# Moving the stationary operands of a float32r matmul stream by multiples of 32 bytes

## The chip, the cores and the metric

The kernel runs on one core of a Trainium2 chip. The metric is device time in microseconds (us) for one execution of the whole program, from the host's launch to its end. The profile has a span of its own, from the first to the last instruction on the core.

## What is computed

Two layers of a streaming encoder on 256 tokens of width 2048, in float32. Each layer has one wide projection, three groups of attention-like heads on parts of it, an output projection, two layer norms and a SwiGLU feed-forward part.

```python
for li in range(DEPTH):                                   # DEPTH = 2, x: (1, 256, 2048)
    proj = x @ w_in[li]                                   # 2048 -> 6920 columns
    ...                                                   # split into the three groups
    ya = diff_attention(qa, ka, va, lam[li], subln_a[li], li)
    yb = chunk_band_attention(qb, kb, vb, rel_bias[li])
    yc = mlstm(qc, kc, vc, oc, ic, fc, conv_w[li], norm_c[li])
    mix = jnp.concatenate([ya, yb, yc], axis=-1) @ w_out[li]
    x = layer_norm(DEEPNORM_ALPHA * x + mix, ln1_g[li], ln1_b[li])
    ffn = (jax.nn.silu(x @ w_gate[li]) * (x @ w_up[li])) @ w_down[li]   # D_FF = 5632
    x = layer_norm(DEEPNORM_ALPHA * x + ffn, ln2_g[li], ln2_b[li])
```

## The kernel before, in words

The four large products (w_in, w_out, w_gate with w_up, w_down) are one long stream of matmuls. `run_groups` cuts it into groups of up to 1024 output columns and each group into steps `k` of 128 rows of the weights. float32 accuracy is kept by splitting each operand in two float32r parts, high and low, and adding three products: high times high, high times low and low times high.

- **Weights (moving operand).** `load_pair` brings two steps at a time from memory into a `raw` tile; `convert` makes the high part `whi` on ScalarE (line 225) and the low part `wlo` on VectorE (line 226). Each has six buffers of 128 partitions x 4096 bytes.
- **Input (stationary operand).** The 256 rows of x, or of the mixed heads, are transposed on TensorE (line 296, `tr_block`) and split by `split` (lines 286 and 287) into `xth` and `xtl`. One pair of tiles holds four steps of 128 rows; `new_xt` (line 290) hands out four slots for each of the two, in turn. So a group of 16 steps uses each slot for four steps in a row.
- **SwiGLU product (stationary operand of w_down).** It lies in `gth` and `gtl`, 24576 bytes per partition each (line 1029), with a tile `gpad` of `G_PAD` float32 ahead of them (line 1028).

Line 273 is the matmul of the stream. A step has, for each of two token halves `t`, three products times two column blocks of 512 (in one group of each layer 512 and 264): twelve matmuls, each with its own weight load of 128 columns. In the rows, `mm<-whi,xth` names first the moving and then the stationary operand. The small matmuls and transposes of attention (`aux` tiles) stand in the same TensorE queue between two steps.

Where tiles lie. Each pool takes a stretch of every partition's bytes, in the order in which the pools are opened: constants, x, the slots of `xth` and `xtl`, then `raw`, `whi`, `wlo`, then small tiles, then the pools of a layer's attention or feed-forward part. Before the change every slot of `xth` and `xtl`, every buffer of `whi` and `wlo`, and `gth` and `gtl` start at 32 modulo 256 bytes. Inside a tile the operands start at multiples of 512 bytes. What is called distance below is the address of the stationary operand less that of the moving operand beside whose matmul it is loaded, modulo 256: in the stream of before it is 0 throughout. The operands of attention lie elsewhere. With `whi` as the matmul's moving operand the distance of the load behind it is 192 for `eT` (line 750), `work` (line 742) and `g_a` (line 493, four columns), 96 for the triangle of ones (line 484), 0 for `x` (line 296), 128 for `mixc` in the first layer and 160 in the second (line 296), and 4 for the `qk` tile that line 626 loads at 352.50 us.

Work that runs beside the stream (evacuations, layer norms, attention's steps) is put between steps by `Tasks`, by fixed costs in the code.

Of the kernel before, what the change touches and what calls it, by code (L numbers as in the profile page):

```python
# [10 lines left out]
F32 = mybir.dt.float32  # L11
F32R = mybir.dt.float32r
# [5 lines left out]
P = 128  # L18
SEQ = 256
# [26 lines left out]
FAR_AHEAD = 4  # L46
EVAC_ACT = (0, 1)
LAST_SKEW = 6
G_PAD = 32
WARM = 9  # L50
MM_BUFS = 5
AUX_BUFS = 3
# [23 lines left out]
class Tasks:  # L76
# [4 lines left out]
    def __init__(self):  # L81
        self.q = []
        self.credit = 0.0
# [52 lines left out]
class Trunk:  # L136
    def __init__(self, tc, ctx, x, w_in, gate_bias, conv_w, lam, subln_a, norm_c, rel_bias, w_out,
                 ln1_g, ln1_b, w_gate, w_up, w_down, ln2_g, ln2_b, cst, out):
        self.tc, self.nc, self.ctx = tc, tc.nc, ctx
        self.__dict__.update(x=x, w_in=w_in, gate_bias=gate_bias, conv_w=conv_w, lam=lam, subln_a=subln_a,  # L140
                             norm_c=norm_c, rel_bias=rel_bias, w_out=w_out, ln1_g=ln1_g, ln1_b=ln1_b,
                             w_gate=w_gate, w_up=w_up, w_down=w_down, ln2_g=ln2_g, ln2_b=ln2_b, cst=cst, out=out)
        self.tasks = Tasks()
        pool = lambda name, bufs=1, **kw: ctx.enter_context(tc.tile_pool(name=name, bufs=bufs, **kw))
        self.const = pool("const")
        self.res = pool("res")
        self.xtp = pool("xtp")
        self.wp = pool("wp")
        self.small = pool("small", bufs=4)
        self.psum = pool("psum", space=bass.MemoryType.PSUM)  # L150
        self.flags = set()
        self.cms = {}


# [132 lines left out]
        self.nc.vector.tensor_tensor(out=lo, in0=ps, in1=hi.bitcast(F32), op=ALU.subtract)  # L287

    def new_xt(self):
        return [self.xtp.tile([P, 4, SEQ], F32R, name=n, tag=n, bufs=4) for n in ("xth", "xtl")]  # L290

    def tr_block(self, srcs, dst, slot0, t):

# [722 lines left out]
    def ffn_groups(self, l):  # L1016
        groups = []
        box = {}
        for hf in range(2):
            blk0 = sum(FF_SPLIT[:hf])  # L1020
            for bi in range(FF_SPLIT[hf]):
# [4 lines left out]
                def start(hf=hf, bi=bi):  # L1026
                    if bi == 0:
                        self.gpool.tile([P, G_PAD], F32, name="gpad")
                        self.gt = [self.gpool.tile([P, KH, SEQ], F32R, name=n, tag=n) for n in ("gth", "gtl")]
# [96 lines left out]
```

## Time and profile before

| | |
|---|---|
| device time, median of 2 runs | 2342.24 us (2341.36 to 2343.12) |
| the profiled execution's own time | 2341.18 us |
| its span | 2339.4 us |
| mean granted TensorE clock | 0.998 |
| matmuls on TensorE, busy | 2318.4 us, 10538 instructions |
| weight loads, busy (they overlap matmuls) | 1905.5 us |
| VectorE, ScalarE, GpSimd busy | 1498.3, 1034.5, 55.1 us |
| DMA | 441.15 MB, mean 189 GB/s |

The busy time of an engine is the union of its instructions' times. Matmuls are pipelined: one starts before the one ahead of it has ended, and the ends are modelled, so the pace is read from starts, and the duration of one matmul moves with the distance from its start to the next. "x2" in a timeline row is two instructions merged. In the groups, "mean ns of one" is the mean duration, then comes the idle time of the engine ahead of them.

### The profile page before, as it was taken

To read this page: it belongs to the slowest core of one execution; us is meant where nothing else is said; L and a number is where in the kernel's file an instruction comes from. 1 tells how busy PE (TensorE), PEld (TensorE's weight loads), DVE (VectorE), ACT (ScalarE), POOL (GpSimd) and SP (SyncE) were. 2 spreads that over 40 slices of the span, in tenths; PEclk is the share of its full clock that TensorE was granted. 3 is DMA by queue.
4 is the path that set the end of the run, shared out by engine and by line. 5 is a ranking of instruction groups with operands and counts; after the bars stand their busy time and mean duration, and the time that the engine had idled before them with its cause. 6 is when DMAs were issued, how large, how long until landed. Compare 5 with 4: busy or idle time off the path is not lost.

```text
span 2339.4 us, 27628 instructions
## 1 busy us (share of the span) xinstructions
PE 2318.4 (99%) x10538; PEld 1905.5 (81%) x10538; DVE 1498.3 (64%) x2360; ACT 1034.5 (44%) x1303; POOL 55.1 (2%) x120
## 2 busy tenths in 40 slices
PE   9999999999999999999999999999999999999997
PEld 7887788888888888888888877888888888888886
DVE  5755455777766447766577454557677664577765
ACT  5645554444444334444345454544444433444432
POOL 0001200000000000000000021000000000000000
PEclk9999999999999999999999999999999999999999
DMA  8654345565555555555556544555655555556553
GB/s 280 202 187 168 133 164 201 185 224 181 194 201 197 196 188 192 186 207 189 177 182 212 182 144 152 172 198 200 209 185 198 198 192 190 193 180 212 184 196 109
DMA packets 178933, 441.15 MB, mean 189 GB/s; under 512 B 15120, under 2 KB 22256, under 8 KB 177776
## 3 DMA queue, kind: packets, MB, share of 16 engines
q1 hardware_dynamic: 178656, 439.32, 55.5%
q8 instruction: 82, 1.34, 0.2%
q14 instruction: 51, 0.42, 0.1%
q10 hardware_dynamic: 144, 0.07, 0.0%
HBM read 437.25 MB, written 2.10 MB: 188 GB/s over the span
## 4 chain that ended last, share of the span: by engine, by line
PE 96%; DVE 2%; POOL 1%; ACT 1%; DMA 0%; issue 0%; SPq 0%; POOLq 0%
PE mm L273 92%; PE aux L296 1%; PE aux L543 1%; PE aux L415 1%; POOL mixc L610 1%; DVE x L341 0%; PE aux L716 0%; PE aux L626 0%; DVE bst L320 0%; DMA raw<-w_in 0%; ACT whi L225 0%; POOL rs L332 0%; POOL ve L330 0%; DVE wlo L226 0%; PE aux L750 0%
## 5 line engine op out<-in xcount | busy, mean ns | idle before, releaser
L226 DVE TENSOR_TENSOR wlo<-raw,whi 128x1024 fp32r<-128x1024 f32 (+2 forms) x817 | 985.8, 1212 | 705.0 <-ACT whi L225 700.9
L225 ACT CAST whi<-raw 128x1024 fp32r<-128x1024 f32 (+2 forms) x817 | 852.6, 1045 | 1172.5 <-PE mm L273 1142.9
L273 PE MATMUL mm<-whi,xth 128*128 128x512 f32 (+1 forms) x2560 | 812.6, 392 | 0.5 <-ACT whi L225 0.3
L273 PE MATMUL mm<-wlo,xth 128*128 128x512 f32 (+1 forms) x2560 | 799.1, 387 | 0.0
L273 PE MATMUL mm<-whi,xtl 128*128 128x512 f32 (+1 forms) x2560 | 798.2, 387 | 0.0
L273 PEld LDWEIGHTS mm<-whi,xtl 128*128 128x128 f32 x2560 | 476.2, 188 | 100.0 <-DVE xtl L287 0.6
L273 PEld LDWEIGHTS mm<-wlo,xth 128*128 128x128 f32 x2560 | 476.5, 188 | 98.8
L273 PEld LDWEIGHTS mm<-whi,xth 128*128 128x128 f32 x2560 | 467.0, 188 | 96.3 <-issue 4.0
L273 PE MATMUL mm<-whi,gtl 128*128 128x512 f32 x704 | 222.0, 389 | 0.0
L273 PE MATMUL mm<-whi,gth 128*128 128x512 f32 x704 | 222.0, 389 | 0.0
L273 PE MATMUL mm<-wlo,gth 128*128 128x512 f32 x704 | 221.9, 389 | 0.0
L407 DVE STREAM_TRANSPOSE gtr<-sil 32x128 f32<-32x128 f32 x704 | 213.0, 303 | 11.2
L273 PEld LDWEIGHTS mm<-whi,gth 128*128 128x128 f32 x704 | 132.1, 188 | 27.7
L273 PEld LDWEIGHTS mm<-whi,gtl 128*128 128x128 f32 x704 | 132.1, 188 | 27.5
L273 PEld LDWEIGHTS mm<-wlo,gth 128*128 128x128 f32 x704 | 132.1, 188 | 27.3
L330 POOL TENSOR_SCALAR ve<-mv 128x1 f32<-128x1 f32 x8 | 4.7, 590 | 1756.6 <-DVE mv L328 1756.5
L286 ACT CAST xth<-aux 128x512 fp32r<-128x512 f32 (+1 forms) x58 | 28.8, 511 | 29.0 <-PE aux L296 25.6
L287 DVE TENSOR_TENSOR xtl<-aux,xth 128x512 fp32r<-128x512 f32 (+1 forms) x58 | 33.5, 592 | 4.3 <-ACT xth L286 4.0
L1088 DVE TENSOR_TENSOR gtl<-gtr,gth 128x512 fp32r<-128x512 f32 x44 | 29.9, 681 | 0.7
L1035 ACT ACTIVATE sil<-mm 128x512 f32<-128x512 f32 x44 | 25.9, 594 | 9.9 <-PE mm L273 9.9
L1038 DVE TENSOR_TENSOR sil<-mm,sil 128x512 f32<-128x512 f32 x44 | 28.2, 682 | 1.4 <-ACT sil L1035 1.4
L341 DVE SCALAR_TENSOR_TENSOR x<-x,rs,lnb 128x512 f32<-128x512 f32 (+1 forms) x40 | 24.7, 639 | 2.8 <-POOL rs L332 2.7
(154 smaller groups left out, 677.1 us busy)
## 6 DMA issues: line engine op xcount, KB each, us to landing
raw<-w_gate SPq DMA_DIRECT2D x176, 512.0 KB, 3.7
raw<-w_up SPq DMA_DIRECT2D x176, 512.0 KB, 4.6
raw<-w_down SPq DMA_DIRECT2D x88, 1024.0 KB, 5.1
raw<-w_in SPq DMA_DIRECT2D x78, 1024.0 KB, 4.9
raw<-w_out SPq DMA_DIRECT2D x32, 1024.0 KB, 5.2
raw<-w_in SPq DMA_DIRECT2D x52, 512.0 KB, 4.1
raw<-w_in SPq DMA_DIRECT2D x16, 256.0 KB, 3.9
lng<-ln_g SPq DMA_DIRECT2D x4, 1024.0 KB, 7.8
```

Source lines behind the costliest of these rows:

```text
L225: nc.scalar.copy(out=hi[:, s], in_=src[:, s])
L226: nc.vector.tensor_tensor(out=lo[:, s], in0=src[:, s], in1=hi[:, s].bitcast(F32), op=ALU.subtract)
L273: nc.tensor.matmul(banks[t, b][:, 0:w], lt, wt[:, o:o + w], start=(k == 0 and i == 0), stop=(k == nk - 1 and i == 2))
L286: self.nc.scalar.copy(out=hi, in_=ps)
L287: self.nc.vector.tensor_tensor(out=lo, in0=ps, in1=hi.bitcast(F32), op=ALU.subtract)
L296: self.nc.tensor.transpose(out=ps[:, i * P:(i + 1) * P], in_=s, identity=self.ident)
L341: nc.vector.scalar_tensor_tensor(out=z, in0=z, scalar=rs, in1=lb[:, s], op0=ALU.mult, op1=ALU.add)
L407: self.nc.vector.transpose(out=out[32 * j:32 * j + 32, 0:n, 32 * i:32 * i + 32], in_=in_[32 * i:32 * i + 32, 0:n, 32 * j:32 * j + 32])
L415: self.nc.tensor.transpose(out=ps[:, i * P:(i + 1) * P], in_=stg[:, i * P:(i + 1) * P], identity=self.ident)
L1035: nc.scalar.activation(out=box["s", t], in_=bank, func=AF.Silu)
L1038: nc.vector.tensor_tensor(out=g, in0=bank, in1=g, op=ALU.mult)
L1088: nc.vector.tensor_tensor(out=lo, in0=gt, in1=hi.bitcast(F32), op=ALU.subtract)
```

## The change

The slots of `xth` and `xtl` become 32 bytes longer each (`XT_PAD` of 8 float32), so that the four slots start 32 bytes apart modulo 256. A tile of 128 bytes that nothing uses is put between the last slot of `xth` and the first of `xtl`. `G_PAD` falls from 32 to 16 float32.

Worked out from the pools' sizes, the slots of `xth`, and those of `xtl`, then start at 32, 64, 96 and 128 modulo 256, `raw`, `whi` and `wlo` at 160, and `gth` and `gtl` at 96. The distances are 128, 160, 192 and 224 for the four slots and 192 for the two parts of the product. In a group the steps 0 to 3, 4 to 7, 8 to 11 and 12 to 15 meet distances 128, 224, 192 and 160. The order of the instructions on every engine, their shapes and what they wait for are the same as before.

```diff
-G_PAD = 32
+G_PAD = 16
+XT_PAD = 8
...
+        self.padded = False
...
     def new_xt(self):
-        return [self.xtp.tile([P, 4, SEQ], F32R, name=n, tag=n, bufs=4) for n in ("xth", "xtl")]
+        out = []
+        for n in ("xth", "xtl"):
+            x = self.xtp.tile([P, 4 * SEQ + XT_PAD], F32R, name=n, tag=n, bufs=4)
+            out.append(x[:, 0:4 * SEQ].rearrange("p (k q) -> p k q", q=SEQ))
+            if n == "xth" and not self.padded:
+                self.padded = True
+                self.xtp.tile([P, 32], F32, name="xpad")
+        return out
```

## Rows read from the trace of the kernel before

**Rows 1.** The page, engines' busy time, and TensorE's granted clock in 40 slices.

```profile
PE 2318.4 (99%) x10538; PEld 1905.5 (81%) x10538; DVE 1498.3 (64%) x2360; ACT 1034.5 (44%) x1303; POOL 55.1 (2%) x120
...
PEclk9999999999999999999999999999999999999999
```

**Rows 2.** Chain of work that ended last, in time: start us, us, what.

```profile
479.13 683.00 PE mm L273 x3012
```

**Rows 3.** Groups by line and shape, whole run: count | busy us, mean ns.

```profile
L273 PE MATMUL mm<-wlo,xth 128*128 128x512 f32 x2496 | 790.7, 390 | 0.0
...
L273 PE MATMUL mm<-whi,gth 128*128 128x512 f32 x704 | 222.0, 389 | 0.0
...
L273 PE MATMUL mm<-wlo,xth 128*128 128x264 f32 x64 | 18.1, 282 | 0.0
```

**Rows 4.** Timeline of TensorE, settled stretch: start us, us, what; first and last.

```profile
1000.07 0.62 PE L273 MATMUL mm<-whi,xth 128*128 128x512 f32 x2
...
1005.51 0.62 PE L273 MATMUL mm<-whi,xth 128*128 128x512 f32 x2
```

**Rows 5.** Groups by line and shape, 500 to 1150 us.

```profile
L273 PE MATMUL mm<-whi,xtl 128*128 128x512 f32 x628 | 196.5, 389 | 0.0
...
L273 PE MATMUL mm<-whi,gth 128*128 128x512 f32 x330 | 102.7, 389 | 0.0
```

**Rows 6.** Timeline of TensorE in the group with 264 columns, first and last.

```profile
65.71 0.51 PE L273 MATMUL mm<-whi,xtl 128*128 128x512 f32 x2
...
67.81 0.39 PE L273 MATMUL mm<-whi,xtl 128*128 128x512 f32 x1
```

**Rows 7.** Timeline of TensorE around one transpose of x.

```profile
29.74 0.62 PE L273 MATMUL mm<-whi,xtl 128*128 128x512 f32 x2
30.20 0.60 PE L296 MATMUL aux<-cst_sb,x 128*128 128x128 f32 x4
30.55 0.71 PE L273 MATMUL mm<-whi,xth 128*128 128x512 f32 x2
31.09 0.62 PE L273 MATMUL mm<-wlo,xth 128*128 128x512 f32 x2
31.56 0.62 PE L273 MATMUL mm<-whi,xtl 128*128 128x512 f32 x2
32.02 0.62 PE L273 MATMUL mm<-whi,xth 128*128 128x512 f32 x2
```

**Rows 8.** Timeline of TensorE, small matmuls that follow a main one.

```profile
119.75 0.28 PE L484 MATMUL aux<-g_lf,cst_sb 128*128 128x4 f32 x2
...
122.71 0.61 PE L273 MATMUL mm<-whi,xtl 128*128 128x512 f32 x2
123.16 0.38 PE L493 MATMUL aux<-cst_sb,g_a 128*4 128x128 f32 x2
...
191.95 0.27 PE L742 MATMUL aux<-cst_sb,work 128*128 128x128 f32 x1
...
199.99 0.38 PE L750 MATMUL aux<-av,eT 128*128 128x128 f32 x2
...
352.50 0.28 PE L626 MATMUL aux<-qk 128*128 128x128 f32 x1
```

**Rows 9.** Groups, 199.94 to 199.97 us: the last main matmul before line 750.

```profile
L273 PE MATMUL mm<-whi,xtl 128*128 128x512 f32 x1 | 0.4, 388 | 0.0
```

**Rows 10.** Groups, 119.69 to 119.73 us: the last main matmul before line 484.

```profile
L273 PE MATMUL mm<-whi,xtl 128*128 128x512 f32 x1 | 0.4, 391 | 0.0
```

**Rows 11.** Groups, 315.16 to 315.19 us: before line 296 on mixc, first layer.

```profile
L273 PE MATMUL mm<-whi,xtl 128*128 128x512 f32 x1 | 0.4, 393 | 0.0
```

**Rows 12.** Groups, 1475.64 to 1475.68 us: before line 296 on mixc, second layer.

```profile
L273 PE MATMUL mm<-whi,xtl 128*128 128x512 f32 x1 | 0.4, 392 | 0.0
```

**Rows 13.** Groups, 191.90 to 191.94 us: the last main matmul before line 742.

```profile
L273 PE MATMUL mm<-whi,xtl 128*128 128x512 f32 x1 | 0.4, 398 | 0.0
```

**Rows 14.** Groups, 352.44 to 352.48 us: the last main matmul before line 626.

```profile
L273 PE MATMUL mm<-whi,xtl 128*128 128x512 f32 x1 | 0.4, 397 | 0.0
```

## The prediction

> **What bounds the kernel now.** I read the page's busy table first: TensorE's matmuls are busy 2318.4 us of a span of 2339.4, at the full 2.4 GHz level in every slice [rows 1]. The chain of work in order of time comes next. It is made of long runs of line 273 alone, such as 3012 matmuls in 683.00 us with nothing between them [rows 2]. No wait of another engine ends last there, so the time is a count of matmuls times a pace, and a change of addresses can only act through the pace.
>
> The count: the groups by line and shape have 2496 + 64 matmuls for wlo with xth and 704 for whi with gth [rows 3]; line 273 runs three such products over each operand. That is 3 x 2560 = 7680 on the input's tiles and 3 x 704 = 2112 on the product's, 9792 in all, of which 192 are 264 columns wide and 9600 are 512 wide.
>
> The pace: in a settled stretch twelve pairs start between 1000.07 and 1005.51 us [rows 4]: 5.44 us / 24 = 226.7 ns from start to start. The long run agrees: 683.00 / 3012 = 226.8 [rows 2]. The mean duration of one is 389 ns for the input's tiles and for the product's alike [rows 5]. Durations overlap, and their ends are modelled; 389 goes with 226.7 between starts, so a matmul read as 393 stood about 4 ns longer. I use differences of durations in that way below.
>
> What in 226.7 ns could depend on an address? In the group with 264 columns, six pairs of one wide and one narrow matmul take 67.81 - 65.71 = 2.10 us [rows 6], 350 ns a pair, so the narrow one has 123.3. The slope is (226.7 - 123.3) / 248 columns = 0.417 ns a column, the 2.4 GHz rate, and 226.7 - 512 x 0.417 = 13.3 ns are left that do not depend on the columns. A weight load runs beside every matmul, so these 13.3 ns are the part on which the distance between the two operands could act. All main matmuls of before have distance 0, so the main loop never shows another one. But the small matmuls of attention do: each time one of them follows a main matmul, its weight load, at some other distance, runs beside the last main matmul.
>
> **The change part by part.** No instruction, wait, shape or transfer is added, removed or moved: the program's order and its waits are the same on all five engines. The instructions of ScalarE and VectorE on these tiles work on other addresses and are hidden under the matmuls as now (the row of 3012 shows no wait on them). What remains is one term, 7680 matmuls at distances 128, 160, 192 and 224 (a quarter, 1920, each) and 2112 at 192.
>
> Distance 192, plain load. Before line 750 at 199.99 us [rows 8] the load of eT lies at 192. The main matmul beside it took 388 ns [rows 9]: no change against 389. Price 0 for one slot and for both parts of the product.
>
> Distance 96, plain load: the triangle's load for line 484 [rows 8] gave 391 [rows 10], 3 ns over 388. This is the nearest plain load to 160 and 224: like them an odd multiple of 32.
>
> Transposes give the other distances, with a shorter kind of load. They must be compared among themselves. At distance 0 two matmuls and the step to the transpose take 30.20 - 29.74 = 0.46 us [rows 7]. At 128 the matmul reads 393 [rows 11], at 160 it reads 392 [rows 12], at 192, before line 742 [rows 8], it reads 398 [rows 13]. The pair at distance 0 gives about 230 a start, thus some 393. So 128 and 160 cost between -1 and 0, and 192 costs 5 in this kind of load and nothing in the plain one.
>
> My values: 128 at 0 (the transposes' row). 192 at 0 (the plain load's row, the same kind as ours). 160 and 224 halfway between the transposes' 0 and the plain 3: 1.5 ns, since 160 has one row of each kind near it and 224 has none of its own. The sum is 3840 x 1.5 ns = 5.8 us. The profiled execution is 2341.18 us, so 2347.0. The median of the two runs is 1.06 above that execution, which makes 2348.
>
> Bounds from the same rows. Below: -1 ns at 160 and 224, 3840 x 1 = 4 us, and the loss after each interruption gone as well. That loss is small: after a transpose some five to six matmuls stand at about 231 before the pace is back at 226.7 [rows 7], and over the whole run the wide matmuls of wlo with xth have a mean of 390 [rows 3] where settled ones have 389 [rows 5], so 1 ns x 7680 = 8 us. That is 2329. Above: 3 for 128 and 160, 5 for 192 and 224, 1920 x (3 + 3 + 5 + 5) = 31 us, and 2112 x 5 = 11 us for the product: 2383.
>
> Whether the 13.3 ns can be won is the larger question. The main matmul before line 493 had a load of four columns beside it, at distance 192, where others have 128 columns. Its pair and the step still take 123.16 - 122.71 = 0.45 us [rows 8]. A load with a thirty-second of the columns at another distance left the pace as it was, so the fixed part does not look like the reading of the load colliding with the matmul's.
>
> [...]
>
> **The rivals.**
>
> (a) Part of the 13.3 ns goes, because at distance 0 the two reads do collide. For it: they are fixed per matmul, and the main loop has never run at another distance. Against it: 388 at 192, and the load of four columns. If all goes, 9792 x 13.3 = 130 us, 2211; if the input's alone, 7680 x 13.3 = 102, 2239; a third of it, 43 us, is close to the 2% line.
>
> [...]
>
> (b) At some distances the matmuls do not settle. After an interruption starts stand at about 231 ns until the pace falls into 226.7 [rows 7]; at distance 0 it always does within some ten matmuls. If at the new distances it never did, 231.3 - 226.7 = 4.6 ns on 9792 are 45 us, 2386; on the odd multiples of 32 alone, 18 us, 2359. This is the slower rival: its place is the two long runs, and it decides against me from 4.8 ns a matmul on (46.8 us / 9792). For it: the unsettled pattern lasts through all of the 264-column group. Against it: that group still averages the same 13.3 ns, and 388 at 192 right after settled matmuls.
>
> (c) A distance prices like the worst plain row: the load for line 626, at distance 4, gave 397 [rows 8, 14], 8 ns over 389; on 9792 matmuls 78 us, 2420. Against it: 4 breaks the 32-byte grid, on which all new distances lie.
>
> (d) Addresses do nothing: 2342. It is inside my forecast's own range.
>
> **How the numbers follow.** Forecast with (d) 0.62, own range 2329 to 2362. (b) 0.20, of which 0.07 beyond 2%. (c) 0.06. (a) 0.12. Two per cent, about what a measurement of this kernel can tell from no change, is 47 us, so the lines are 2295 and 2389. Faster 0.12. Slower 0.07 + 0.06 = 0.13. Within 0.62 + 0.13 = 0.75. The range 2325 to 2395 takes in the bounds and nearly all of (b); it leaves out (a) and (c), some 0.18.
>
> **What would show it.** A mean of 389 in the grouped view for line 273 over the long runs, for xth, xtl, gth and gtl, and pairs 0.453 us apart in the timeline, would show the forecast right. Each slot serves four steps of 12 matmuls in a row, so in a block of the feed-forward part four stretches of 48 matmuls show their distances apart: 128 and 192 should have 226.7, 160 and 224 up to 230. Pairs near 0.46 throughout are (b); pairs at 0.44 or below are (a). A wait of line 273 for ScalarE or VectorE that is not there now would show that an address changed those engines, which I have costed at nothing; to matter they would have to use up the slack that the run of 3012 hides. My forecast is wrong above all if one load at another distance does not speak for thousands in a row.

## The result and the profile after

| | before | after |
|---|---|---|
| device time, median of 2 runs | 2342.24 us | 2381.46 us (2380.87 to 2382.05) |
| span of the profiled execution | 2339.4 us | 2379.1 us |
| matmuls on TensorE, busy | 2318.4 us | 2360.2 us |
| mean granted TensorE clock | 0.998 | 0.997 |

The ratio is 1.0169, with a 95% interval from 1.015 to 1.0188: 39 us slower, inside 2% and clear of no change. The forecast of "within 2%" and the range of 2325 to 2395 held. The forecast's own 2348, with its range of 2329 to 2362, did not: the time came out where the slower rival (b) had it, 2386, and near the upper bound of the terms, 2383.

The chain of work in order of time, after (start us, us, what), beside [rows 2]:

```profile
59.66 33.03 PE mm L275 x186
...
486.20 696.17 PE mm L275 x3012
...
1666.10 692.05 PE mm L275 x2994
```

The run of 3012 matmuls took 683.00 us before and takes 696.17 now, 231.1 ns a matmul for 226.8. It is still one unbroken run of the same matmuls, so the loss is in the pace and not in a wait. The stretch of 186 matmuls with the 264-column blocks took 32.89 us before and takes 33.03: it hardly changed.

The groups by line and shape over the whole run, after, beside [rows 3] (count | busy us, mean ns of one | idle ahead):

```profile
L275 PE MATMUL mm<-whi,xth 128*128 128x512 f32 x2496 | 815.9, 400 | 0.6 <-ACT whi L227 0.4
L275 PE MATMUL mm<-whi,xtl 128*128 128x512 f32 x2496 | 802.1, 394 | 0.0
L275 PE MATMUL mm<-wlo,xth 128*128 128x512 f32 x2496 | 801.6, 394 | 0.0
L275 PE MATMUL mm<-whi,gtl 128*128 128x512 f32 x704 | 224.7, 393 | 0.0
L275 PE MATMUL mm<-wlo,gth 128*128 128x512 f32 x704 | 223.4, 391 | 0.0
L275 PE MATMUL mm<-whi,gth 128*128 128x512 f32 x704 | 222.7, 390 | 0.0
```

Before, the three forms on the input had 395, 390 and 390 ns, and those on the product 389. So the input's wide matmuls cost 2496 x (5 + 4 + 4) = 32 us more and the product's 704 x (4 + 2 + 1) = 5 us: 37 of the 39.7 us by which the span grew. The idle time ahead of them is 0.6 us as against 0.5, so no wait has appeared that could explain the loss. The weight loads read 188 ns in both traces: a load itself takes no longer in the changed kernel.

Where in the slots the loss lies is read from one feed-forward block of the changed kernel, in four windows: 1010 to 1020 us at distance 192, 1021 to 1031 at 160, 1032 to 1042 at 128, and 1043 to 1053 at 224. One row of the groups from each, in that order:

```profile
L275 PE MATMUL mm<-whi,xtl 128*128 128x512 f32 x14 | 4.3, 391 | 0.0
...
L275 PE MATMUL mm<-whi,xtl 128*128 128x512 f32 x15 | 5.0, 395 | 0.0
...
L275 PE MATMUL mm<-whi,xtl 128*128 128x512 f32 x14 | 4.4, 395 | 0.0
...
L275 PE MATMUL mm<-whi,xtl 128*128 128x512 f32 x15 | 4.8, 395 | 0.0
```

Three distances cost 6 ns a matmul (395) over the 389 of before [rows 5], and 192 costs about 2 (391). The timeline has the pace itself. At 192, from start to start:

```profile
1010.55 0.62 PE L275 MATMUL mm<-whi,xtl 128*128 128x512 f32 x2
...
1019.71 0.62 PE L275 MATMUL mm<-wlo,xth 128*128 128x512 f32 x2
```

and at 128:

```profile
1032.31 0.63 PE L275 MATMUL mm<-wlo,xth 128*128 128x512 f32 x2
...
1041.64 0.63 PE L275 MATMUL mm<-whi,xth 128*128 128x512 f32 x2
```

Forty matmuls take 9.16 us at 192 and 9.33 us at 128: 229.0 and 233.3 ns where [rows 4] have 226.7.

### The profile page after: what moved, and what is told of

Same layout as the page of the kernel before. It is cut to its first block, busy times and chain, and to the rows that moved or that the text cites. A ratio compares the mean times of both kernels' runs of the same rounds, so it can differ in the third digit from the quotient of the medians.

```text
span 2379.1 us, 27628 instructions
## 1 busy us (share of the span) xinstructions
PE 2360.2 (99%) x10538; PEld 1908.0 (80%) x10538; DVE 1500.6 (63%) x2360; ACT 1032.5 (43%) x1303; POOL 54.7 (2%) x120
## 4 chain that ended last, share of the span: by engine, by line
PE 96%; DVE 2%; POOL 1%; ACT 1%; DMA 0%; issue 0%; SPq 0%; POOLq 0%
PE mm L275 92%; PE aux L305 1%; PE aux L552 1%; PE aux L424 1%; DVE x L350 0%; POOL mixc L619 0%; PE aux L725 0%; PE aux L635 0%; DVE bst L329 0%; DMA raw<-w_in 0%; DVE wlo L228 0%; POOL ve L339 0%; ACT whi L227 0%; PE aux L759 0%; POOL rs L341 0%
## 5 line engine op out<-in xcount | busy, mean ns | idle before, releaser
L227 ACT CAST whi<-raw 128x1024 fp32r<-128x1024 f32 (+2 forms) x817 | 850.1, 1042 | 1212.5 <-PE mm L275 1182.4
L275 PE MATMUL mm<-whi,xth 128*128 128x512 f32 (+1 forms) x2560 | 824.4, 397 | 0.6 <-ACT whi L227 0.4
L275 PE MATMUL mm<-whi,xtl 128*128 128x512 f32 (+1 forms) x2560 | 810.5, 392 | 0.0
L275 PE MATMUL mm<-wlo,xth 128*128 128x512 f32 (+1 forms) x2560 | 810.0, 391 | 0.0
```

Of the source, the lines that this page charges most:

```text
L227: nc.scalar.copy(out=hi[:, s], in_=src[:, s])
L275: nc.tensor.matmul(banks[t, b][:, 0:w], lt, wt[:, o:o + w], start=(k == 0 and i == 0), stop=(k == nk - 1 and i == 2))
```

## The experiments

Theory A is that the pace hangs on the distance between the stationary tile being loaded and the moving tile being streamed, modulo 256. Its rivals are B (the residue itself counts, above all that of the weights, which moved from 32 to 160) and C (the loss comes where one distance gives way to the next). The times of before beside these runs are 2341.5 to 2341.9 us. Unless another kernel is named, a diff is against the kernel before.

**The second part undone.** Against the changed kernel:

```diff
-G_PAD = 16
+G_PAD = 32
```

> The changed kernel with its second part undone: G_PAD 32 puts the product back at distance 0 from the weights, the slots stay at 128 to 224. If the parts add up, the product's 2112 matmuls go back from 228.9 to 226.7 ns, 4.7 us less than the changed kernel's 2381.5: 2376.8 us, a ratio to the kernel before of 1.0148. If the product's part were the costly one, the time would fall to near 2342.

Measured: 2377.43 us, 1.0151 of before (1.0134 to 1.0168). That leaves 4 us for the product and 35 for the slots; the parts add up. The intervals of this run and of the change overlap, so the product's part is read from its rows, which are back at 389 and 390 from 390 to 393. Between 500 and 1150 us:

```profile
L275 PE MATMUL mm<-whi,gtl 128*128 128x512 f32 x300 | 93.6, 390 | 0.0
```

**All residues moved, distances kept at 0.**

```diff
+        self.nx = 0
...
     def new_xt(self):
+        if self.nx == 0:
+            self.xtp.tile([P, 32], F32, name="xpad")
+        self.nx += 1
```

> The kernel before with 128 unused bytes ahead of the first slot: inputs, weights and product all lie at 160 modulo 256, distance 0 everywhere. Theory A (the distance between the stationary tile being loaded and the moving tile being streamed sets the pace): 226.7 ns a matmul as before, 2342 us. Theory B (the residue itself counts: the weights moved from 32 to 160 in the changed kernel, and 160 is a worse place to stream from): about the changed kernel's pace, 229 to 233 ns, 2370 us or more.

Measured: 2341.26 us, 0.9998 of before (0.9989 to 1.0008). Its long run in the chain of work is that of before to 0.01 us:

```profile
479.15 682.99 PE mm L274 x3012
```

B falls: weights at 160 cost nothing here (2341.26 us) with the stationary tiles there too.

**One distance for everything, 160.**

```diff
-G_PAD = 32
+G_PAD = 8
...
+        self.nx = 0
...
-        return [self.xtp.tile([P, 4, SEQ], F32R, name=n, tag=n, bufs=4) for n in ("xth", "xtl")]
+        out = [self.xtp.tile([P, 4, SEQ], F32R, name=n, tag=n, bufs=4) for n in ("xth", "xtl")]
+        if self.nx == 0:
+            self.xtp.tile([P, 24], F32, name="xpad")
+        self.nx += 1
+        return out
```

> The kernel before with 96 unused bytes between slots and weights, and 8 float32 ahead of the product: every load has distance 160, and nothing ever changes from one distance to another. Theory A: the pace that distance 160 showed in the changed kernel, 233.4 ns, on all 9792 matmuls: 9792 x 6.7 ns = 66 us over before, 2408 us, a ratio of 1.028. Theory C (the loss comes where the distance changes from one slot to the next, because the matmuls have to settle again): no slot changes the distance here, so 226.7 ns and 2342 to 2346 us.

Measured: 2398.19 us, 1.0241 of before (1.0225 to 1.0256). C falls: no distance changes here, and the loss is larger than that of the change. Its chain of work:

```profile
60.23 33.22 PE mm L274 x186
...
488.17 702.88 PE mm L274 x3012
```

702.88 / 3012 = 233.4 ns, the pace that A gave for the settled runs. A's 2408 was still 10 us too high, because it put 6.7 ns on every matmul. Matmuls that were not settled before had less to lose. From the starts of the same matmuls in both traces, the 8415 wide ones that stood 225 to 228 ns from the next before lose 6.7 ns each, and the 1045 other wide ones 1.4. The stretch with the 264-column blocks went from 32.89 to 33.22 us only, 1.8 ns a matmul; half of its matmuls are narrow, and these lose 1 ns.

**The other four distances.** Slots 32 bytes longer, as in the change, with 128 unused bytes behind the slots of xth and behind those of xtl; the product stays at 0.

```diff
...
+            x = self.xtp.tile([P, 4 * SEQ + 8], F32R, name=n, tag=n, bufs=4)
+            out.append(x[:, 0:4 * SEQ].rearrange("p (k q) -> p k q", q=SEQ))
+            if self.nx == 0:
+                self.xtp.tile([P, 32], F32, name="xpad" + n)
...
```

> Slots at distances 0, 32, 64 and 96, product at 0. Theory A says nothing of which distance costs what; if a distance and its negative cost the same, 32 goes as 224 (233.3 ns), 64 as 192 (229.0) and 96 as 160 (233.4), and the slot at 0 keeps 226.7: some 1870 matmuls each x (0 + 6.6 + 2.3 + 6.7) = 29 us, 2371 us. Theory B: the weights are back at 32, so 2342 us whatever the slots.

Measured: 2376.53 us, 1.0148 of before (1.0133 to 1.0163), 6 us over the 2371 that the symmetry would give, and B's 2342 falls once more. In one block, the windows 1008 to 1018 us (distance 64), 1019 to 1029 (32), 1030.5 to 1040 (0) and 1041.5 to 1051.5 (96), one row each:

```profile
L274 PE MATMUL mm<-whi,xth 128*128 128x512 f32 x16 | 5.0, 396 | 0.0
...
L274 PE MATMUL mm<-whi,xtl 128*128 128x512 f32 x15 | 5.0, 396 | 0.0
...
L274 PE MATMUL mm<-whi,xth 128*128 128x512 f32 x16 | 4.9, 390 | 0.0
...
L274 PE MATMUL mm<-whi,xth 128*128 128x512 f32 x15 | 4.8, 397 | 0.0
```

Of these four only 0 keeps the pace. A distance and its negative do not cost the same: 64 costs what 32 does (396 both), and 192 does not (391 in the changed kernel). In this kernel the slots of xtl start 16640 bytes behind those of xth (4 slots of 4128 bytes and the 128 unused ones), 65 turns of 256; at 0 both parts show 390, so these whole turns of 256 cost no more than 1 ns.

**Off the grid of 32 bytes.** The same layout with the data shifted in the slots by 16, 4, 8 and 16 bytes, which makes the distances 16, 100, 72 and 48.

```diff
...
+        o = (4, 1, 2, 4)[self.nx % 4]
...
+            out.append(x[:, o:o + 4 * SEQ].rearrange("p (k q) -> p k q", q=SEQ))
...
```

> Slots at distances 16, 48, 72 and 100, product at 0: is there a distance, off the 32-byte grid, under 226.7 ns? Theory A with reads of 32 bytes: 16 and 48 cost as much as their 32-byte neighbours or more (229 to 238 ns), none under 226.7; 2370 to 2390 us. If the 13.3 ns that stand over 512 columns are a collision that some distance avoids, one of the four slots shows less than 226.7 ns.

Measured: 2375.17 us, 1.0142 of before (1.0122 to 1.0162). In the windows 1018.5 to 1028.5 us (48), 1030 to 1040 (16) and 1041 to 1051 (100):

```profile
L274 PE MATMUL mm<-wlo,xth 128*128 128x512 f32 x15 | 5.0, 397 | 0.0
...
L274 PE MATMUL mm<-wlo,xth 128*128 128x512 f32 x15 | 4.8, 395 | 0.0
...
L274 PE MATMUL mm<-wlo,xth 128*128 128x512 f32 x15 | 4.7, 392 | 0.0
```

None is under 389, and the time lies in the 2370 to 2390 that was expected. 100 is as good as 192 (392 and 391), though it is no multiple of 16; 48 (397), 72 (396) and, in this block, 16 (395) are as bad as the rest. The reads of 32 bytes in the expectation are an assumption that no run shows.

**A map of distances.** Blocks of 48 further matmuls at the end, 29 lines of this kind. Each of the two maps is one execution, and no other engine works beside the blocks.

```diff
+        hi, lo = self.whl[max(self.whl)]
...
+        for i in range(48): nc.tensor.matmul(ps, lo[:, 0:128], hi[:, 0:512], start=True, stop=True)
+        for i in range(48): nc.tensor.matmul(ps, lo[:, 4:132], hi[:, 0:512], start=True, stop=True)
...
+        for i in range(48): nc.tensor.matmul(ps[0:64, 0:512], lo[:, 0:64], hi[:, 0:512], start=True, stop=True)
...
```

> The kernel before, unchanged, with 29 blocks of 48 further matmuls at its end whose results nothing reads: the moving operand is whi, the stationary one a slice of wlo, so that any distance can be had. Sixteen blocks at 0, 16, ..., 240; then 4, 8, 36 and 256; one with both operands moved by 32 bytes; then loads of 64 and of 32 columns, and moving widths of 384 and 256, each at 0 and at 160. Theory A: 226.7 ns at 0, at 256 and with both moved; 233.3 at 160; 229 at 192; no distance under 226.7. Theory D (the load's reads meet the stream's reads in the same part of the memory, two to three times per load of 512 bytes, and each meeting costs 16 cycles): the 13.3 ns shrink with the load: about 220 ns with 64 columns and 217 with 32, at 0. Theory E (the 13.3 ns are a fixed price of a matmul of this type, and only what stands over them depends on addresses): 226.7 at distance 0 whatever the load's columns.

From start to start of the blocks in the timeline, divided by 48, in ns: 226.7 at 0, 226.9 at 16, 233.1 at 32 and 64, 233.3 at 48, 112, 128, 144, 160, 208 and 224, 231.7 at 80, 234.2 at 96, 229.8 at 176, 229.0 at 192, 227.1 at 240 (with its settling); 232.5 at 4, 230.8 at 8, 234.4 at 36; 227.3 at 256 and 227.3 with both operands moved by 32 bytes. Rows of the timeline for 0, 16, 32 and 192 (the second row of a pair starts the next block), then for a load of 64 columns and of 32 at distance 0:

```profile
2326.89 11.04 PE L1097 MATMUL aux<-whi,wlo 128*128 128x512 f32 x48
2337.77 11.05 PE L1098 MATMUL aux<-whi,wlo 128*128 128x512 f32 x48
2348.66 11.35 PE L1099 MATMUL aux<-whi,wlo 128*128 128x512 f32 x48
2359.85 11.36 PE L1100 MATMUL aux<-whi,wlo 128*128 128x512 f32 x48
...
2460.43 11.15 PE L1109 MATMUL aux<-whi,wlo 128*128 128x512 f32 x48
2471.42 11.36 PE L1110 MATMUL aux<-whi,wlo 128*128 128x512 f32 x48
...
2560.03 11.21 PE L1118 MATMUL aux<-whi,wlo 128*64 128x512 f32 x48
2571.07 11.27 PE L1119 MATMUL aux<-whi,wlo 128*64 128x512 f32 x48
2582.18 11.28 PE L1120 MATMUL aux<-whi,wlo 128*32 128x512 f32 x48
2593.30 11.35 PE L1121 MATMUL aux<-whi,wlo 128*32 128x512 f32 x48
```

A's 0, 160 and 192 come out as forecast, and so do 256 and both moved, but for the settling at a block's start. 16 does not agree with the run before it, which had 395 there: 226.9 here is the settled pace. No distance of the map is under 226.7. D falls: with a load of 64 columns the matmuls take 11.04 / 48 = 230.0 ns and with 32 columns 231.7, more than with 128. Its meetings of 16 cycles are an assumption, and no run shows them. E falls in its letter too, since 226.7 is not kept. At 256 columns of moving width, 0 and 160 are alike (119.8 and about 120), at 384 they are 173.5 and 176.7, at 512 226.7 and 233.3: what distance 160 costs depends on the width.

**Only the low part moved.** xth and the product stay at distance 0, xtl lies at 160.

```diff
...
+        for n, w in (("xth", 40), ("xtl", 24)):
+            out.append(self.xtp.tile([P, 4, SEQ], F32R, name=n, tag=n, bufs=4))
+            if self.nx == 0:
+                self.xtp.tile([P, w], F32, name="xpad" + n)
...
```

> The kernel before with 160 unused bytes between xth and xtl and 96 behind xtl: xth and the product stay at distance 0, xtl lies at 160. In each half step of six matmuls two loads of xtl run beside a wlo and a whi matmul, the four others at distance 0. If each load prices for itself: one third of the input's matmuls at 6.7 ns, 2500 x 6.7 = 17 us, 2359 us. If two loads at another distance keep the matmuls from settling: 5 to 6 ns on all of the input's 7500, some 40 us, 2380 us.

Measured: 2379.01 us, 1.0163 of before (1.0146 to 1.018). That is the second theory's 2380, and not the 2359 of a price for each load. Its groups between 500 and 1150 us:

```profile
L274 PE MATMUL mm<-whi,xth 128*128 128x512 f32 x638 | 203.9, 396 | 0.0
L274 PE MATMUL mm<-whi,xtl 128*128 128x512 f32 x640 | 203.2, 393 | 0.0
L274 PE MATMUL mm<-wlo,xth 128*128 128x512 f32 x638 | 203.1, 394 | 0.0
L274 PE MATMUL mm<-whi,gth 128*128 128x512 f32 x302 | 94.2, 389 | 0.0
```

The matmuls of whi with xth lost most (396), though every load beside them was at distance 0. By starts, in the two long runs, a matmul of the input with a load at 0 beside it stands 232.2 ns from the next on average, and one with a load at 160 stands 233.7. Two loads in six at another distance kept all six from the settled 226.7. So the loss here is not a price for each load; that it is a state of the stream is a reading of these numbers.

**A second map: widths, shorter loads, and what ran before.** The same kind of blocks, 33 of them.

> The kernel before with 33 blocks of 48 further matmuls at its end whose results nothing reads, whi as the moving and slices of wlo as the stationary operand. Moving widths at distance 160, and two at 0. Theory F (13.3 ns are fixed per matmul, and out of the settled state one cycle more is lost per 16 columns beyond the first 256): 134 ns for 288 columns, 148 for 320, 163 for 352, 191 for 416, 205 for 448 and 219 for 480 at distance 160; at distance 0 width / 2.4 + 13.3, 147 and 200 for 320 and 448. Theory G (one more fixed price per matmul as soon as the stream outlasts the load): 13.3 + 6.7 ns over the columns for every width above 256 at 160, 140 ns for 288. Then loads of 112, 96 and 16 columns at 0: 226.7 only for 128 columns if the settled state hangs on the load's own length. Then distances 12, 20, 24, 244, 248 and 252: near 226.7 or not says how wide the good zone around 0 is. Then 16 and 240 behind blocks at 160, 128, 192 and 0: 226.7 behind all of them if the distance alone decides, and a different pace by what ran before if the state of the two streams does.

Measured at distance 160: 131.7 ns for 288 columns, 146.7 for 320, 162.3 for 352, 193.3 for 416, 205.2 for 448, 219.8 for 480; at distance 0: 146.7 for 320 and 202.5 for 448. G falls (140 for 288). F is near, within 2.5 ns, but what it should explain is itself small: 160 costs nothing over 0 at 320 columns, 2.7 ns at 448 and 6.6 at 512. At 448 columns distance 0 does not give F's 200 either. 288 columns at 160 take 11.7 ns over 288 / 2.4, less than the 13.3 that F holds to be fixed. Loads of 112, 96 and 16 columns at 0: 229.0, 230.0, 229.0. Distances 12, 20, 24, 244, 248, 252: 230.0, 233.3, 231.0, 233.3, 233.1, 226.9. So of the distances tried the good ones are single (0, 240, 252 and at times 16: 226.7 to 227.1), not a zone. Blocks at 16, the first behind a block at 160, the second behind one at 128 (timeline, with the row that starts the next block):

```profile
2505.22 11.05 PE L1115 MATMUL aux<-whi,wlo 128*128 128x512 f32 x48
2516.11 11.37 PE L1116 MATMUL aux<-whi,wlo 128*128 128x512 f32 x48
...
2549.35 11.36 PE L1119 MATMUL aux<-whi,wlo 128*128 128x512 f32 x48
2560.55 11.32 PE L1120 MATMUL aux<-whi,wlo 128*128 128x512 f32 x48
```

The same 48 matmuls take 10.89 us (226.9 ns) behind one block and 11.20 us (233.3 ns) behind the other. Behind blocks at 192 and at 0 the matmuls at 16 take 226.7. So at 16 both paces occur, by the block that ran before: A, in the strict form that the distance alone sets the pace, falls here. 240 came out at about 226.8 behind all four.

## Why the prediction was right, and where it was not

**The bound and the absence of waits: right.** The chain is the same run of the same matmuls, line 275 for 273 by numbering. ScalarE only waits longer for TensorE: 1182.4 us in all ahead of its conversions for 1142.9 before.

**The 13.3 ns that stand over the columns: right that they stay.** The test of rival (a) is the two maps: none of their distances goes under 226.7. What I concluded from the load of four columns, that this part is not the reading of the load, agrees with loads of 16 to 112 columns, which made no matmul faster (229.0 to 231.7 ns). The prediction's 2.4 GHz is the slope of its rows, 0.417 ns a column or 2.4 columns a ns; the profile gives the granted clock only as a share, 0.998. The working behind the 13.3 was loose: it gave the wide matmuls of the 264-column group the settled 226.7, and by their starts in the trace of before they stand 230.0 from the next there and the narrow ones 120.0. The first map bears the 13.3 out without that group: at distance 0, 119.8 at 256 columns and 173.5 at 384 are 13.1 and 13.5 over width / 2.4. That nothing of it is won is shown for 512 columns and the distances of the maps only: 288 columns at 160 had 11.7.

**The price at 192: the step that failed is one reading for a cycle.** I took 0 from a single 388 ahead of line 750 [rows 9]. In the changed kernel three matmuls in a row at 192, from 1013 us on, read:

```profile
L275 PE MATMUL mm<-wlo,xth 128*128 128x512 f32 x1 | 0.4, 392 | 0.0
...
L275 PE MATMUL mm<-whi,xtl 128*128 128x512 f32 x1 | 0.4, 394 | 0.0
...
L275 PE MATMUL mm<-whi,xtl 128*128 128x512 f32 x1 | 0.4, 388 | 0.0
```

388 is the lowest of a cycle of three whose mean is 391. The 388 of before came right behind settled matmuls, as the first one at a new distance, and said nothing of the ones that would follow. Another reading of that kind would have been no better, as the rows of the next paragraph show. The measured price is 2.3 ns, not 0.

**The prices at 128, 160 and 224: the step that failed is the kind of load.** I took 0 for 128 from a transpose (393 against some 393 at distance 0, [rows 11]), 1.5 for 160 and 224. They measured 6.6 each. The second map has single plain loads behind settled matmuls: the last matmul of a block runs beside the first load of the next one. Ahead of the blocks at 160, at 128 and at 192, at 2516.06, 2538.14 and 2582.54 us and each time at the end of a settled block (at 16, 240 and 240), it reads:

```profile
L1115 PE MATMUL aux<-whi,wlo 128*128 128x512 f32 x1 | 0.4, 397 | 0.0
...
L1117 PE MATMUL aux<-whi,wlo 128*128 128x512 f32 x1 | 0.4, 396 | 0.0
...
L1121 PE MATMUL aux<-whi,wlo 128*128 128x512 f32 x1 | 0.4, 388 | 0.0
```

One plain load at 160 or at 128 cost 8 or 7 ns at once over the settled 389, and the first one at 192 nothing. The transposes could not show this: behind settled matmuls of 389 those of x read mostly 392 and 393 at distance 0 already, and [rows 11] and [rows 12] have the same at 128 and 160, so their shorter load (140 to 142 ns, a plain one 188) does not stand for a plain one. The prediction said that it would be wrong above all "if one load at another distance does not speak for thousands in a row". That is what happened at 192. Added up from the starts of the same matmuls in the traces of before and after, the slots at 128, 160 and 224 lost about 32 us, the one at 192 4 and the product 5; the sum had 5.8, 0 and 0.

**Rival (b) is what happened.** I gave it 0.20 and priced it at 231.3 ns, from the stretch behind a transpose [rows 7]. The measured paces are 233.3 for three slots and 229.0 for the fourth and the product. 2386 was 5 us over the time: the wide matmuls that were unsettled before lost 0.8 ns each, and the settled ones 4.7. The argument against it, 388 at 192, was the failed reading. [rows 7] were the better evidence: they show that one distance, 0, has a fast and a slow pace (226.7 and about 231). With that I should have asked which distances can hold the fast one, not what a load at a distance costs.

**What was luck.** The forecast's own range missed the time by 19 us. "Within 2%" came true because rival (b), at the distances that this change happens to give, cost 1.7%: with 160 for everything the loss is 2.4%. Nothing in the sum had chosen between the two.

**Rival (c)** did not come: 2420 would have needed 8 ns on every matmul. The dearest distances of the map, 36 and 96, cost 7.7 and 7.5, and distance 4, from which (c) had its 8 ns, costs 5.8 in a run of 48.

**Rival (d), that addresses do nothing, falls.** The kernel with everything at 160 differs from before in addresses alone and takes 1.0241 of its time. Whether the two reads of TensorE get in each other's way is not shown: no trace shows a read that waits.

**What stays open.** Why the pace over a settled 226.7 is lost is not shown. The runs show that the pace differs with the distance (226.7 ns at 0, 233.3 at 160), the loss at 160 with the moving width (0 at 320 columns, 6.6 ns at 512), and the pace with the load's length (226.7 with 128 columns, 231.7 with 32, at 0) and with what ran before (226.9 or 233.3 at 16). F gives the intervals at 160 within 2.5 ns, where the loss itself is 0 to 7. The loads read 188 ns in the changed kernel as they do in the one before, so the trace puts the loss on the matmuls and does not say what holds them. I have no mechanism that gives the list of good distances.

## What to carry to other kernels

Where loads and matmuls alternate without a gap, and the matmuls are float32r of 512 columns, as here, put the stationary and the moving operands at the same residue modulo 256 bytes; it costs a pad tile at most. Both at 32 and both at 160 gave 2341 to 2342 us here. The kernels with other residues took 1.4 to 2.4% longer, and with a third of the input's loads at another residue (1.6% longer) the matmuls beside the others stood 232.2 ns apart and not 226.7. Where the settled pace of a long run stands as one repeated interval, a change of addresses can only be judged by a run of dozens at the new address: a single matmul there can read as the best of a cycle, as 388 of 392, 394 and 388 did. And a price read beside one kind of load need not hold for another: at 160 it was 392 beside a transpose's and 397 beside a plain one. A cheap way to get such runs is to append blocks of matmuls whose results nothing reads, as the maps did.

## What the runs showed of the hardware that was not expected

- The stream of float32r matmuls of 512 columns had a settled pace of 226.7 ns and an unsettled one of 229 to 234, by the distance between its two operands (226.7 at 0, 233.3 at 160). The granted clock did not move (0.996 to 0.998 in all of the timed kernels).
- A shorter load did not help: 230.0 ns with 64 columns, 231.7 with 32, 229.0 with 16, as against 226.7 with 128, all at distance 0.
- At 16 bytes of distance the same matmuls ran at 226.9 or at 233.3 ns, by the block that came ahead of them.
- Between distances 0 and 160 there was no difference at 256 columns of moving width (119.8 and about 120 ns) and at 320 (146.7 both); at 512 it was 6.6 ns.
- Behind settled matmuls the first load at 192 cost nothing (388 ns) and the first at 128 or 160 cost 7 or 8 ns (396 and 397).
